# A hybrid encoder block on one core: next stage's factors made under the last products, tiles placed for that, one accumulator

## The chip, the cores and the metric

The kernel runs on one core of a Trainium2 chip. The metric is the device time of one execution in microseconds. Before the change it is 3190.73 us, the median of three executions (3188.22 to 3192.93).

The engines of a core work side by side, each on its own list of instructions in a fixed order: PE multiplies matrices, DVE, ACT and POOL work on elements, and SP's queue issues DMA transfers. An instruction waits until what it reads is written and what it overwrites has been read; everything behind it on its engine waits too.

## The reference

One layer of an encoder on a stream x of 2048 rows by 1024 columns, all in float32:

```python
xn = rmsnorm(h, g_pre_mix)
p = xn @ w_in                                   # 1024 -> 4608 columns
y_a = spatial_gating(gelu(p_a), ...) @ w_out_a   # gMLP in chunks of 128 rows
y_b = hyena_mixer(p_b, ...) @ w_out_b            # two long convolutions by FFT
m = (sigmoid(g_a) * y_a + sigmoid(g_b) * y_b) @ w_o
h = h + rmsnorm(m, g_post_mix)
hn = rmsnorm(h, g_pre_ffn)
f = square(relu(hn @ w_ff1)) @ w_ff2             # 1024 -> 4096 -> 1024
h = h + rmsnorm(f, g_post_ffn)
```

The change touches the last four lines, and the layout in which the result of the second convolution is stored.

## The kernel before

Every float32 product is made of three matmuls: each factor is split into a high part that PE takes at full rate (`_h`, a cast on ACT, line 36) and the rest (`_l`, a subtraction on DVE, line 42), and `mm3` (lines 47 to 49) adds h·h, l·h and h·l. The two halves together are called a factor here, and making them is called cutting it.

Four stages follow one another.
- Input projection, filters, FFT convolutions and gMLP, up to about 1434 us. The second convolution leaves its result in DRAM as `z2d`.
- **Merge**, to about 1765 us: for each of 8 blocks b of 256 rows, `project(b)` (products with w_out_b, gating) and then the products with w_o (tile `mo`). The rows are normalised, added to x on POOL, written to `hd`, normalised again (`rows_in`, tile `mx_n`, line 928), transposed by PE (`ta`, line 933), copied by ACT (`xb`), combined by DVE and written to `xtd`. The work on one block's rows is queued in the list `late` and interleaved with the next block's products; what is left for b = 7 runs at the end.
- **Up** (hn @ w_ff1), 33 steps s to about 2479 us. It uses a scheme of seven products in place of eight for 2x2 blocks. The right factors x[1..7] (`xh`, `xl`, from `xtd`) stay for 16 steps (q = s // 16 is the half of the rows), the left factors come from a pair of weight columns, one `raw8` buffer of 1 MB a step, by sums and differences. One product is 4 x 3 matmuls of 128x512 into one PSUM bank. Results (squared relu) are written to `sd`.
- **Down** (@ w_ff2), to about 3150 us: for c = 0..7 and n = 0..6 four products r = 0..3 of 12 matmuls, `s` (from `sd`) by `t` (from weight blocks `wr`). With c // 4 the half of the rows changes. At c % 4 = 0 ACT copies the bank into `acc[n, r]` (line 1244), later DVE adds (line 1246). After c % 4 = 3 `finish` combines the seven accumulators (line 1254), squares on ACT (1270), multiplies by the gain on POOL (1271), makes the reciprocal root by a chain of small DVE instructions, adds the rows of `hd` (1277) and writes `out` (1278).

The loads that matter go through SP: `load8` takes one of three 1 MB `raw8` buffers, for weight pairs, right factors and `sd` alike. A scheduler sets the order on each engine when the program is built, from the order of the code and the dependencies; a pool's tile waits for the last reader of the tile that held its memory before. In the up stage the right factors lie in pool `xc`, left ones in `fs` (5 buffers), rows in `fr`; the down stage opens its pools where those were.

Of the kernel before, what the change touches and what calls it, by code (L numbers as in the profile page):

```python
# [26 lines left out]
class Kernel:  # L27
# [174 lines left out]
    def prologue(self):  # L202
# [10 lines left out]
        self.gpm = load("gpm", [128, 8])  # L213
        dt = lambda name, shape, t=F32: d.tile(shape, t, name=name)
# [3 lines left out]
        self.z2d = dt("z2d", [4, 128, 32, 64])  # L218
# [326 lines left out]
    def gen_fft(self):  # L545
# [74 lines left out]
        for o in range(2):  # L620
# [76 lines left out]
            for j in range(18 if o == 0 else 16):  # L697
# [10 lines left out]
                if j < 16:  # L708
# [14 lines left out]
                    nc.vector.tensor_tensor(xi, y, xi, op=OP.mult)  # L723
                    zo[j] = xi
                    if o == 0:
                        late.append(lambda j=j, xi=xi: nc.sync.dma_start(
                            self.z1d[j].rearrange("p t n -> p (t n)"), xi))
                    else:
                        late.append(lambda j=j, xi=xi: nc.sync.dma_start(
                            self.z2d[:, :, 2 * j:2 * j + 2, :].rearrange("t p a n -> p t (a n)"), v4(xi)))  # L730
# [124 lines left out]
    def merge(self, st3):  # L855
# [9 lines left out]
        wsp = E("mw", 2)  # L865
        c = E("mc", 1)
# [3 lines left out]
        mtp = E("mt", 2)  # L870
        gpf = self.bcast(E("mf", 1), "gpf")
# [49 lines left out]
        def rows_in(b, i, x, bt):  # L921

            j = mp.tile([128, D], BF16, name="mx_j", bufs=1)
# [4 lines left out]
            nc.vector.scalar_tensor_tensor(xs, x, r, gpf, op0=OP.mult, op1=OP.mult)  # L928

            def turn(j):  # L930
# [5 lines left out]
                nc.scalar.copy(t, p)  # L936
                bt[j, i] = t
            late.append(lambda: turn(0))
            late.append(lambda: turn(1))
# [3 lines left out]
        def sums(b, bt):  # L943

            t1, t2, t4 = [xp.tile([128, Q], F32, name=f"xs{n}") for n in range(3)]
            sub = lambda o, a, c: nc.vector.tensor_tensor(o, a, c, op=OP.subtract)
            b11, b12, b21, b22 = bt[0, 0], bt[0, 1], bt[1, 0], bt[1, 1]
            sub(t1, b12, b11)
            sub(t2, b22, t1)
            sub(b12, b22, b12)  # L950
            sub(t4, b21, t2)
            c = slice((b % 4) * 128, (b % 4) * 128 + 128)
            for n, t in enumerate((b11, b21, t2, b12, t1, t4, b22)):
                nc.sync.dma_start(self.xtd[b // 4][n][:, :, c], t.rearrange("p (k n) -> p k n", k=4))
# [41 lines left out]
        for f in late:  # L996
            f()
# [441 lines left out]
```

## Time and profile before

| | us |
|---|---|
| median of three executions | 3190.73 (3188.22 to 3192.93) |
| the profiled execution | 3195.43 |
| its span in the trace | 3193.7 |
| PE busy in the span | 2890.2 (90%) |
| DVE busy | 2271.3 (71%) |
| ACT busy | 1523.4 (48%) |
| mean granted clock of PE | 0.961 |

A timeline row gives the start (us from the span's start), the time taken, the engine, the line of the kernel, the operation, output<-input tiles, and in brackets how long the engine had been idle and who released it. PE's matmuls overlap, so one that takes 0.39 us may start 0.23 us after the one before. The granted clock is a share of the full 2.4 GHz; 0.5 is the lower level of 1.2 GHz.

### The profile page before, as it was taken

To read this page: it belongs to the slowest core of one execution; us is meant where nothing else is said; L and a number is where in the kernel's file an instruction comes from. 1 tells how busy PE (TensorE), PEld (TensorE's weight loads), DVE (VectorE), ACT (ScalarE), POOL (GpSimd) and SP (SyncE) were. 2 spreads that over 40 slices of the span, in tenths; PEclk is the share of its full clock that TensorE was granted. 3 is DMA by queue.
4 is the path that set the end of the run, shared out by engine and by line. 5 is a ranking of instruction groups with operands and counts; after the bars stand their busy time and mean duration, and the time that the engine had idled before them with its cause. 6 is when DMAs were issued, how large, how long until landed. Compare 5 with 4: busy or idle time off the path is not lost. (4 is left out here: it accounts for less than half of the span.)

```text
span 3193.7 us, 37066 instructions
## 1 busy us (share of the span) xinstructions
PE 2890.2 (90%) x12910; PEld 2315.1 (72%) x12910; DVE 2271.3 (71%) x3532; ACT 1523.4 (48%) x2335; POOL 380.6 (12%) x324
## 2 busy tenths in 40 slices
PE   7999899998999899998999599968999799969994
PEld 5777766777777677787777488856888588848883
DVE  6589867777775866847776566656666567895788
ACT  4466555666535666324443444444444433334332
POOL 1122310211211211210111000000000000030002
PEclk9999999999999999999999799988999899979997
DMA  8556566454697454598866444444444544444332
GB/s 312 187 192 215 183 219 204 150 166 137 228 308 252 136 171 155 191 256 267 224 202 199 157 154 152 151 140 154 153 150 156 201 164 149 150 178 158 147 119 92
DMA packets 310952, 581.11 MB, mean 182 GB/s; under 512 B 58213, under 2 KB 147685, under 8 KB 292589
## 3 DMA queue, kind: packets, MB, share of 16 engines
q1 hardware_dynamic: 286348, 500.10, 47.3%
q10 hardware_dynamic: 19152, 61.35, 6.0%
q0 software_dynamic: 5264, 17.31, 1.4%
q8 instruction: 101, 1.65, 0.2%
q14 instruction: 87, 0.70, 0.1%
HBM read 385.72 MB, written 192.94 MB: 181 GB/s over the span
## 5 line engine op out<-in xcount | busy, mean ns | idle before, releaser
L36 ACT CAST s_h<-raw 128x512 fp32r<-128x512 f32 (+1 forms) x248 | 225.6, 911 | 539.5 <-PE mm L48 511.7
L47 PE MATMUL mm<-xh,w_hi 128*128 128x512 f32 x1152 | 459.8, 400 | 6.0 <-ACT xh L36 3.0
L48 PE MATMUL mm<-xl,w_hi 128*128 128x512 f32 x1152 | 457.3, 397 | 2.6 <-DVE xl L42 2.6
L49 PE MATMUL mm<-xh,w_lo 128*128 128x512 f32 x1152 | 457.8, 398 | 0.0
L47 PE MATMUL mm<-xh,s_h 128*128 128x512 f32 x896 | 360.1, 402 | 41.7 <-ACT xh L36 41.7
L47 PE MATMUL mm<-t_h,s_h 128*128 128x512 f32 x896 | 350.9, 393 | 36.0 <-ACT t_h L36 23.0
L48 PE MATMUL mm<-xl,s_h 128*128 128x512 f32 x896 | 360.6, 403 | 11.2 <-DVE xl L42 11.2
L48 PE MATMUL mm<-t_l,s_h 128*128 128x512 f32 x896 | 351.5, 392 | 18.2 <-DVE t_l L42 18.2
L42 DVE TENSOR_TENSOR s_l<-raw,s_h 128x512 fp32r<-128x512 f32 (+1 forms) x248 | 259.7, 1048 | 141.3 <-ACT s_h L36 141.0
L49 PE MATMUL mm<-xh,s_l 128*128 128x512 f32 x896 | 358.4, 400 | 0.0
L49 PE MATMUL mm<-t_h,s_l 128*128 128x512 f32 x896 | 351.1, 392 | 0.0
L47 PEld LDWEIGHTS mm<-xh,w_hi 128*128 128x128 f32 x1152 | 219.9, 191 | 60.1 <-ACT xh L36 5.4
L48 PEld LDWEIGHTS mm<-xl,w_hi 128*128 128x128 f32 x1152 | 219.7, 191 | 53.1 <-issue 4.5
L49 PEld LDWEIGHTS mm<-xh,w_lo 128*128 128x128 f32 x1152 | 219.5, 191 | 46.8 <-issue 2.0
L47 PEld LDWEIGHTS mm<-xh,s_h 128*128 128x128 f32 x896 | 172.4, 192 | 85.4 <-ACT xh L36 45.3
L1097 DVE TENSOR_TENSOR r<-r,mm 128x512 f32<-128x512 f32 x160 | 109.9, 687 | 164.4 <-PE mm L49 163.0
L47 PEld LDWEIGHTS mm<-t_h,s_h 128*128 128x128 f32 x896 | 170.1, 190 | 72.4 <-ACT t_h L36 23.4
L48 PEld LDWEIGHTS mm<-xl,s_h 128*128 128x128 f32 x896 | 172.3, 192 | 54.8 <-DVE xl L42 14.7
L1271 POOL TENSOR_TENSOR acc<-acc,gpo 128x512 f32<-128x512 f32 x32 | 49.0, 1558 | 1353.6 <-ACT pn_j L1270 1351.7
L48 PEld LDWEIGHTS mm<-t_l,s_h 128*128 128x128 f32 x896 | 169.8, 190 | 54.8 <-DVE t_l L42 19.3
L49 PEld LDWEIGHTS mm<-xh,s_l 128*128 128x128 f32 x896 | 172.7, 193 | 40.1
L49 PEld LDWEIGHTS mm<-t_h,s_l 128*128 128x128 f32 x896 | 169.7, 189 | 35.4
(274 smaller groups left out, 5762.1 us busy)
## 6 DMA issues: line engine op xcount, KB each, us to landing
sd<-r SPq DMA_DIRECT2D x224, 256.0 KB, 3.8
raw<-sd SPq DMA_DIRECT2D x56, 1024.0 KB, 4.8
w_raw<-in_win_dram ACTq DMA_DIRECT2D x101, 512.0 KB, 3.8
raw<-in_wf_dram SPq DMA_DIRECT2D x32, 1024.0 KB, 6.3
wr<-in_wf_dram SPq DMA_DIRECT2D x32, 1024.0 KB, 5.6
sk<-fs SPq DMA_DIRECT2D x64, 256.0 KB, 2.7
sf<-z_s SPq DMA_DIRECT2D x64, 256.0 KB, 3.5
z_raw<-sf SPq DMA_DIRECT2D x64, 256.0 KB, 2.8
```

The source lines that it names most:

```text
L36: nc.scalar.copy(hi, src)
L42: e.tensor_tensor(lo, src, hi.bitcast(F32), op=OP.subtract)
L47: mm(ps, a[0], b[0], start=start, stop=False, **kw)
L48: mm(ps, a[0], b[1], start=False, stop=False, **kw)
L49: mm(ps, a[1], b[0], start=False, stop=stop, **kw)
L1097: add = lambda o, a, b: nc.vector.tensor_tensor(o, a, b, op=OP.add)
L1271: nc.gpsimd.tensor_tensor(c[e], c[e], gpo[:, es], op=OP.mult)
```

## The change

- `ffn_start`, which runs under the last products of the merge, now also loads and cuts the first right factor (into a pool `x1` of its own) and two left ones. The work on the rows of b = 7 leaves the merge: `last_rows`, a generator run in steps 2 to 5 of up, loads the rows from `hd` again, normalises them, transposes them and writes `xtd`.
- The gain `g_pre_ffn` is applied after the transpose, by ACT, four copies of 128x128 with a scale (`gained`); before the transpose DVE multiplies by the root alone.
- In up, right factors of the first half are cut one by one ahead of the products that need them, those of the second half each after its last product in step 15 (4 and 3 in step 16). The pool `fs` has 3 buffers instead of 5.
- In down, `s` and `t` alternate between pools of one buffer placed on the right and left, and there is one `acc` tile. The additions of the combination follow the products from which they can be made (`ends`), the row-set (5, 4) is finished after n = 5 for all r, (1, 6) after n = 6 in pairs of r, one chain for the root for a batch. For the last half of the rows the (1, 6) finish works without POOL (`tail`).
- `z2d` is laid out so that the merge reads whole rows of 4 KB per partition; its writes are two of 256 B pieces instead of one of 512 B.

```diff
-        self.z2d = dt("z2d", [4, 128, 32, 64])
+        self.z2d = dt("z2d", [4, 128, 2, 32, 32])
...
-                    nc.sync.dma_start(zrs[-1][:, t], self.z2d[t, :, :, 8 * b:8 * b + 32])
+                    nc.sync.dma_start(zrs[-1][:, t], self.z2d[t, :, b // 4])
...
-            nc.vector.scalar_tensor_tensor(xs, x, r, gpf, op0=OP.mult, op1=OP.mult)
+            nc.vector.tensor_scalar(xs, x, r, None, op0=OP.mult)
...
-                nc.scalar.copy(t, p)
+                self.gained(t, p, j)
...
-                rows_in(b, i, x, bt)
+                if b < 7:
+                    rows_in(b, i, x, bt)
...
-        for f in late:
-            f()
...
+    def gained(self, t, p, j):
+        for k in range(4):
+            ks = slice(k * 128, k * 128 + 128)
+            self.nc.scalar.activation(t[:, ks], p[:, ks], AF.Copy, scale=self.gpf[:, 4 * j + k:4 * j + k + 1])
...
-        self.fs = R(self.fs_st, "fs", 5)
-        self.pairs = {}
+        self.x1p = R(self.fs_st, "x1", 1)
+        self.fs = R(self.fs_st, "fs", 3)
+        self.pairs, self.facs, self.x = {}, {}, {}
         self.load_pair(0)
         yield
+        self.xcut(self.x1p, 0, 1)
+        self.need(0, 1)
+        yield
+        self.load_pair(1)
+        self.need(0, 2)
+
+    def xcut(self, pool, p, i):
+        raw = self.load8(self.xtd[p][self.AT[i]], [128, 4, Q])
+        x = self.x[p, i] = pool.tile([128, 4, Q], F32R, name=f"xh{i}"), pool.tile([128, 4, Q], F32R, name=f"xl{i}")
+        self.split(*x, raw)
...
+        def last_rows():
+            raw = self.load8(self.hd[3][256:512, :].rearrange("(i p) d -> p i d", p=128), [128, 2, D])
...
+                        nc.tensor.transpose(p[:, k * 128:(k + 1) * 128], raw[:, i, ds], self.ident)
+                    bt[j, i] = row()
+                    self.gained(bt[j, i], p, j)
+                yield
+            self.sums(7, bt, [row() for n in range(3)])
...
+            nxt = lambda i: xcut(1, i) if s == 15 else None
+            if s == 2:
+                rows = last_rows()
+            next(rows, None)
             if s < 32:
-                if new:
-                    xcut(s // 16, 1)
                 d["a"] = bank()
-                product(d["a"], need(s, 1)[0], 1, True)
+                product(d["a"], need(s, 1)[0], q, 1, True)
+                nxt(1)
...
+            if s == 0:
+                xcut(0, 6)
             if s > 0:
-                product(st[s - 1]["c"], need(s - 1, 7)[5], 4, False)
+                self.load_pair(s + 1)
+                product(st[s - 1]["c"], need(s - 1, 7)[5], (s - 1) // 16, 4, False)
+                if s == 16:
+                    xcut(1, 4)
...
-        acc_p, sp, tp = E("acc", 1), E("sp", 2), E("tp", 2)
+        R = lambda name, bufs: E(name, bufs, side="right")
+        tp, sp = [R("tpa", 1)], [E("spa", 1)]
         wr = E("wr", 5)
+        sp.append(E("spb", 1))
+        tp.append(E("tpb", 1))
+        acc = E("acc", 1).tile([128, 7, 4, Q], F32, name="acc")
...
+        ends = {0: ((1, 0), (2, 0)), 2: ((3, 2), (6, 2)), 3: ((5, 3),), 4: ((6, 4), (4, 3))}
...
-                if c % 4 == 3 and n == 6:
-                    self.finish(acc, gpo, c // 4, r)
+                if last:
+                    for o, x in ends.get(n, ()):
+                        add(a(o), a(o), a(x))
+                    if n == 6 and r % 2 == 1:
+                        self.finish(acc, gpo, g, 0, (r - 1, r), g == 1)
+            if last and n == 5:
+                self.finish(acc, gpo, g, 1, range(4), False)
...
+                if not tail:
+                    nc.gpsimd.tensor_tensor(acc[:, at[e], r, :], acc[:, at[e], r, :], gpo[:, e * Q:e * Q + Q], op=OP.mult)
...
+                if tail:
+                    nc.vector.scalar_tensor_tensor(a, a, rd[:, m:m + 1], gpo[:, es], op0=OP.mult, op1=OP.mult)
+                    nc.vector.tensor_tensor(h[:, es], a, h[:, es], op=OP.add)
+                else:
+                    nc.vector.scalar_tensor_tensor(h[:, es], a, rd[:, m:m + 1], h[:, es], op0=OP.mult, op1=OP.add)
```

PE's order from the merge into up, before (`mo` is the product with w_o, `ta` a transpose, `mm` the first product of up):

```order
L47 MATMUL mo<-wo_h,mt_h 128x512
L933 MATMUL ta<-ident,mx_n 128x128 x4
L48 MATMUL mo<-wo_l,mt_h 128x512
L49 MATMUL mo<-wo_h,mt_l 128x512
L933 MATMUL ta<-ident,mx_n 128x128 x12
L47 MATMUL mm<-xh_16657,s_h 128x512
```

And after the change:

```order
L47 MATMUL mo<-wo_h,mt_h 128x512
L48 MATMUL mo<-wo_l,mt_h 128x512
L49 MATMUL mo<-wo_h,mt_l 128x512
L47 MATMUL mm<-xh_16517,s_h 128x512
L48 MATMUL mm<-xl_16518,s_h 128x512
L49 MATMUL mm<-xh_16517,s_l 128x512
```

The transposes of the last rows no longer stand between the two stages. SP's queue behind the last step of up, before (`raw8` loads of `sd` and `wr` are the factors of down, `nt_x` rows for its finish):

```order
L852 DMA gpo2_21724<-in_gpo2_dram 128x1024
L1265 DMA nt_x_23608<-hd0_122 128x1024
L1265 DMA nt_x_23637<-hd0_122 128x1024
L1021 DMA raw8_21813<-sd003_143 128x2048
L1094 DMA sd134_193<-r_21684 128x512
L1094 DMA sd132_191<-r_21685 128x512
L1094 DMA sd133_192<-r_21516 128x512
L1094 DMA sd136_195<-r_21686 128x512
L1021 DMA raw8_21882<-sd004_144 128x2048
L1207 DMA wr_21728<-in_wf2_dram 128x2048
```

And after:

```order
L1054 DMA raw8_21859<-sd002_144 128x2048
L1120 DMA sd135_196<-r_21730 128x512
L1120 DMA sd131_192<-r_21774 128x512
L859 DMA gpo2_21841<-in_gpo2_dram 128x1024
L1260 DMA wr_21845<-in_wf2_dram 128x2048
L1260 DMA wr_21849<-in_wf2_dram 128x2048
L1120 DMA sd134_195<-r_21794 128x512
```

The first two `wr` loads now follow the load of `gpo2` at once, which waits for the last product of up. DVE's order in the last step of c = 3, before (`pn_` tiles are the chain for the root):

```order
L1246 TENSOR_TENSOR acc_21756<-mm_23587,acc_21756 128x512
L1246 TENSOR_TENSOR acc_21756<-mm_23666,acc_21756 128x512
L1254 TENSOR_TENSOR acc_21756<-acc_21756 128x512 x5
L1273 TENSOR_TENSOR pn_s1_23617<-pn_ss_23610 128x1
L1254 TENSOR_TENSOR acc_21756<-acc_21756 128x512
L72 TENSOR_SCALAR pn_a_23619<-pn_s1_23617 128x1
L1246 TENSOR_TENSOR acc_21756<-mm_23745,acc_21756 128x512
```

And after:

```order
L42 TENSOR_TENSOR s_l_23790<-raw8_23651,s_h_23789 128x2048
L1301 TENSOR_TENSOR acc_21831<-mm_23797,acc_21831 128x512
L42 TENSOR_TENSOR t_l_23792<-wr_23653,t_h_23791 128x2048
L1301 TENSOR_TENSOR acc_21831<-mm_23811,acc_21831 128x512
L1058 TENSOR_TENSOR wr_23653<-wr_23939,wr_23653 128x2048
L1323 TENSOR_TENSOR pn_s4_23744<-pn_ss4_23719 128x4
L1301 TENSOR_TENSOR acc_21831<-mm_23867,acc_21831 128x512
```

The factors of the next half's first step (`s_l`, `t_l`) now stand among the last additions, and the additions of the combination are gone from there.

## Rows read from the trace of the kernel before

**Rows 1.** The profile's page, part 1: each engine's busy time, its share and its instructions.

```profile
PE 2890.2 (90%) x12910; PEld 2315.1 (72%) x12910; DVE 2271.3 (71%) x3532; ACT 1523.4 (48%) x2335; POOL 380.6 (12%) x324
```

**Rows 2.** `windows` view: stretch, its length, each engine's busy time (instructions), clock, DMA share, GB/s.

```profile
1750.00:1850.00 100.00, 66.87 (x257) 51.84 (x256) 62.71 (x111) 41.12 (x58) 5.47 (x4) 0.83 0.51 170
2000.00:2100.00 100.00, 100.00 (x432) 81.05 (x431) 66.17 (x101) 49.52 (x83) 0.00 (x0) 1.00 0.44 147
2100.00:2200.00 100.00, 63.49 (x231) 48.48 (x230) 52.64 (x64) 39.19 (x51) 0.00 (x0) 0.76 0.45 150
2450.00:2550.00 100.00, 76.78 (x324) 62.03 (x323) 47.97 (x39) 41.20 (x47) 0.00 (x0) 0.88 0.58 206
2600.00:2700.00 100.00, 100.00 (x442) 82.80 (x442) 72.61 (x59) 33.45 (x18) 0.00 (x0) 1.00 0.45 166
2800.00:2900.00 100.00, 69.03 (x283) 56.06 (x282) 78.02 (x137) 41.51 (x61) 25.25 (x15) 0.83 0.52 189
3150.00:3193.00 43.00, 0.50 (x3) 0.08 (x1) 36.12 (x109) 7.23 (x20) 16.14 (x13) 0.53 0.50 171
```

**Rows 3.** Timeline of PE around the merge's end: start, length, line, tiles, count, [wait before <-releaser].

```profile
1779.91 1.94 PE L933 MATMUL ta<-ident,mx_n 128*128 128x128 f32 x8 [14.61 <-DVE mx_n L928]
1791.70 0.80 PE L47 MATMUL mm<-xh,s_h 128*128 128x512 f32 x1 [5.97 <-ACT xh L36]
```

**Rows 4.** Timeline of PE in the middle of the up stage.

```profile
2142.49 0.80 PE L47 MATMUL mm<-xh,s_h 128*128 128x512 f32 x1 [14.56 <-ACT xh L36]
```

**Rows 5.** Groups by form on ACT and DVE (busy, mean ns | idle before), and DMA issues of the page.

```profile
L36 ACT CAST xh<-raw 128x2048 fp32r<-128x2048 f32 x14 | 26.5, 1894 | 26.6 <-DMA raw<-xt 26.6
...
L42 DVE TENSOR_TENSOR t_l<-wr,t_h 128x2048 fp32r<-128x2048 f32 x56 | 128.8, 2301 | 14.9 <-ACT t_h L36 14.9
L1025 DVE TENSOR_TENSOR wr<-wr 128x2048 f32<-128x2048 f32 x32 | 72.7, 2282 | 0.2
...
raw<-sd SPq DMA_DIRECT2D x56, 1024.0 KB, 4.8
```

**Rows 6.** Timelines of PE, SP's queue and ACT between up and down.

```profile
2501.61 2.08 PE L47 MATMUL mm<-t_h,s_h 128*128 128x512 f32 x4 [22.96 <-ACT t_h L36]
...
2492.39 2.03 SPq L1207 DMA_DIRECT2D wr<-in_wf_dram  x4
...
2499.66 1.90 ACT L36 CAST t_h<-wr 128x2048 fp32r<-128x2048 f32 x1 [17.11 <-DMA wr<-in_wf_dram]
```

**Rows 7.** Timelines of PE, DVE and POOL in the middle of down.

```profile
2839.38 0.79 PE L48 MATMUL mm<-t_l,s_h 128*128 128x512 f32 x1 [17.93 <-DVE t_l L42]
2865.56 0.80 PE L47 MATMUL mm<-t_h,s_h 128*128 128x512 f32 x1 [13.04 <-ACT acc L1244]
...
2818.76 1.79 DVE L1254 TENSOR_TENSOR acc<-acc 128x512 f32<-128x512 f32 x1
...
2820.81 0.68 DVE L1254 TENSOR_TENSOR acc<-acc 128x512 f32<-128x512 f32 x1
...
2814.51 5.49 POOL L1271 TENSOR_TENSOR acc<-acc,gpo 128x512 f32<-128x512 f32 x4 [0.61 <-ACT pn_j L1270]
```

**Rows 8.** Timelines of PE (its last matmul) and SP's queue at the end.

```profile
3150.11 0.39 PE L49 MATMUL mm<-t_h,s_l 128*128 128x512 f32 x1
...
3158.59 3.03 SPq L1278 DMA_DIRECT2D out_dram<-nt_x  x4
...
3187.08 3.68 SPq L1278 DMA_DIRECT2D out_dram<-nt_x  x4
```

**Rows 9.** Timeline of PE in the merge, and groups by form on DVE.

```profile
1440.76 0.38 PE L47 MATMUL mm<-zq_h,wb_hi 128*128 128x256 f32 x1 [3.26 <-ACT wb_hi L36]
...
1652.15 0.66 PE L933 MATMUL ta<-ident,mx_n 128*128 128x128 f32 x4 [1.58 <-DVE mx_n L928]
...
L928 DVE SCALAR_TENSOR_TENSOR mx_n<-mx,mx_y,gpf 128x1024 f32<-128x1024 f32 x16 | 20.5, 1284 | 1.7 <-DVE mx_y L67 0.2
...
L423 DVE TENSOR_SCALAR f_hd<-f_hd 128x512 f32<-128x512 f32 x8 | 3.4, 426 | 0.5
```

More of the change, by code (lines that the diff above doesn't have):

```diff
@@ L213, in prologue @@
         self.gpm = load("gpm", [128, 8])
+        self.gpf = load("gpf", [128, 8])
         dt = lambda name, shape, t=F32: d.tile(shape, t, name=name)
@@ L943, in sums @@
         def sums(b, bt):
[L945 to L954, printed above, removed]
+            self.sums(b, bt, [xp.tile([128, Q], F32, name=f"xs{n}") for n in range(3)])
         for b in range(8):
@@ L1120, in end_3 @@
             put(s, 3, n4)
-        facs = {}
-        def need(s, n):
-            if s < 32:
-                g = facs.setdefault(s, [self.left(s), []])
-                while len(g[1]) < n:
-                    g[1].append(next(g[0]))
-                return g[1]
+        def last_rows():
+            raw = self.load8(self.hd[3][256:512, :].rearrange("(i p) d -> p i d", p=128), [128, 2, D])
+            bt, s = {}, self.small.tile([128, 2], F32, name="lr_s")
+            for i in range(2):
+                j = rp.tile([128, Q], F32, name="r").bitcast(BF16)
+                nc.scalar.activation(j, raw[:, i], AF.Square, accum_out=s[:, i:i + 1])
+            r = self.rstd(self.small, s, 2, D, "lr")
+            for i in range(2):
+                nc.vector.tensor_scalar(raw[:, i], raw[:, i], r[:, i:i + 1], None, op0=OP.mult)
+            yield
+            for j in range(2):
+                for i in range(2):
+                    p = bank()
+                    for k in range(4):
+                        ds = slice((4 * j + k) * 128, (4 * j + k + 1) * 128)
+                        nc.tensor.transpose(p[:, k * 128:(k + 1) * 128], raw[:, i, ds], self.ident)
+                    bt[j, i] = row()
+                    self.gained(bt[j, i], p, j)
+                yield
+            self.sums(7, bt, [row() for n in range(3)])
+            yield
+        rows = iter(())
         for s in range(33):
+            q = s // 16
             new = s % 16 == 0 and s < 32
             d = st.setdefault(s, {})
-            self.load_pair(s + 1)
+            nxt = lambda i: xcut(1, i) if s == 15 else None
+            if s == 2:
+                rows = last_rows()
+            next(rows, None)
             if s < 32:
-                if new:
-                    xcut(s // 16, 1)
                 d["a"] = bank()
-                product(d["a"], need(s, 1)[0], 1, True)
+                product(d["a"], need(s, 1)[0], q, 1, True)
+                nxt(1)
                 d["u2"] = row()
@@ L1168, in up @@
             need(s, 4)
-            if new:
-                xcut(s // 16, 7)
+            if s == 0:
+                xcut(0, 5)
             d["c"] = bank()
-            product(d["c"], need(s, 4)[3], 7, True)
+            product(d["c"], need(s, 4)[3], q, 7, True)
+            nxt(7)
             d["u3"] = row()
@@ L1186, in up @@
             need(s, 6)
-            need(s + 1, 1) if s + 1 in self.pairs or s + 1 in facs else None
+            need(s + 1, 1)
+            if s == 0:
+                xcut(0, 3)
             need(s, 7)
@@ L1222, in cut @@
             src = (w(0, 0), w(1, 0), wraw.get((c, 2, 2)), wraw.get((c, 0, 1)), w(0, 0), w(1, 0), wraw.get((c, 1, 1)))[n]
-            s = sp.tile([128, 4, Q], F32R, name="s_h"), sp.tile([128, 4, Q], F32R, name="s_l")
-            t = tp.tile([128, 4, Q], F32R, name="t_h"), tp.tile([128, 4, Q], F32R, name="t_l")
+            s = [sp[k % 2].tile([128, 4, Q], F32R, name="s_" + x) for x in "hl"]
+            t = [tp[k % 2].tile([128, 4, Q], F32R, name="t_" + x) for x in "hl"]
             self.split(*s, sraw.pop(k))
@@ L1234, in down @@
             cut(k + 1)
-            if c % 4 == 0 and n == 0:
-                old, acc = acc, acc_p.tile([128, 7, 4, Q], F32, name="acc")
+            g, last = c // 4, c % 4 == 3
             s, t = fac.pop(k)
```

135 lines of the change are left out of this document (70 added, 65 removed).

## The prediction, made before the changed kernel ran

> **What bounds the kernel now.** I read the page's first part, then the windows, then the timelines at the places where the windows show PE short of work. PE is busy 90% of the span [rows 1], and in a full stretch nothing else limits it: 432 matmuls in 100 us of the up stage (0.231 us each), 442 in the down stage (0.226 us) [rows 2]. So the change can win only where PE runs short. There are five such places, and matmuls missing against a full stretch give their size [rows 2]:
> - merge to up: 432 - 257 = 175, by 0.231 us = **41 us**
> - middle of up, where the second half of the rows begins (s = 16): 432 - 231 = 201, **46 us**
> - up to down: 28.7 us at the one rate and 71.3 us at the other would be 439; 324 ran: 115, **26 us**
> - middle of down (c = 4): 442 - 283 = 159, **36 us**
> - tail: PE ends at 3150.5 [rows 8], the span at 3193.7: **43 us**
>
> Together 192 us. They hold the slow clock too: the granted clock is 0.76 to 0.88 there and 1.00 in full stretches [rows 2]. PE falls to its lower level after a wait and pays on after it (after the wait of 22.96 us four matmuls take 2.08 us [rows 6]).
>
> **Merge to up.** PE waits 14.61 us for the last block's normalised rows (mx_n), then 5.97 us for the first right factor [rows 3]; smaller waits for the next factors follow. The change takes the transposes of block 7 out of this place, cuts the first right and left factors under the last merge products, and PE goes from the last mo matmul into the first product. What is late next: the other six right factors. The raw8 pool has three 1 MB buffers, two hold pairs of weights, so five of the six loads pass through one buffer, each issued when the factor before it is cut. A round is a load of 4.8 us or a little more, a cast of 1.89 us and a subtraction of 2.3 us [rows 5]: 9 to 10.4 us. The second of these loads also stands on SP behind the two writes of hd3, which wait for POOL's last addition, some 6 us after the last mo matmul. Factor 2 is then whole at about 16 us, 7 at 26, 5 at 36, 4 at 47, and the ninth product ends at about 56 us, where nine products of 12 x 0.231 = 2.77 us are 25 us: 31 us lost, and some 2 us more for the clock. From 41 to 33: **gain 8** (3 to 14). The rows of block 7 are normalised in steps 2 to 5 instead: their 16 transposes are the same work, and the second half alone reads them.
>
> **Middle of up.** Now all seven factors are cut in the new half's first step; the longest wait is 14.56 us [rows 4]. In the new order factor i is cut as soon as its last product of the old half is done, over steps 15 and 16. The same round of about 10 us applies, but seven rounds (70 us) now have nearly two steps (14 products, 39 us) and the next step's first products to hide in. Followed through the order, factors 1, 6, 2 and 7 come before their products, 5 about 1 us late, 4 and 3 some 2 to 5 us each: 7 to 11 us, with the clock 8 to 16. From 46 to 12: **gain 34** (30 to 39).
>
> **Up to down.** PE waits 22.96 us; the weight loads (wr) are issued at 2492.39, 14 us after PE stopped, since they stand on SP's queue behind gpo2, two row loads, a raw load and the last writes of sd; t_h starts at 2499.66 [rows 6]. After: the pools are placed so that s_h, s_l are made early, but SP holds wr behind the load of gpo2, and that waits for the last up product. So wr is issued about 1 us after it, is usable 5 to 7.3 us later (the page's load; 2492.39 to 2499.66), cast 1.9 us: 8 to 10 us of wait in place of 22.96, and the same clock after it. **Gain 14** (8 to 18). Had the gpo2 load not stood there, the whole wait would be gone; that is the price of its place.
>
> **Middle of down.** PE waits 17.93 us for t_l, then 13.04 us for acc copies [rows 7]: DVE is finishing the first half of the rows, and the copies into the one acc tile wait for that. The change spreads 28 additions of 0.68 us [rows 7] over steps 0 to 4 of c = 3, and finishes two row-sets in three batches. In the steps with eight additions DVE has 2 x 2.3 + 4 x 0.68 + 8 x 0.68 = 12.8 us against PE's 48 x 0.226 = 10.8, so it comes some 2 us late by the end of c = 3. Then, from the end of step 5 to the t_l of c = 4, n = 2, DVE has 8 additions from PSUM (5.4), six subtractions for factors (13.8), three on weights (6.8), three small chains (3.5), four STT (3.0): 32.5 us. That equals PE's three steps, 32.5 us. What breaks the tie is POOL: its 16 multiplications run there. In the trace an addition takes 1.79 us while POOL is multiplying and 0.68 after it [rows 7]: 1.1 us per multiplication, 17 us in all. So about 17 us are lost in place of 36: **gain 19** (10 to 28). The copies of acc 1 wait, as before, for rows loaded through two buffers; by the order they come in time.
>
> The Trainium skill (SBUF — State Buffer, Who interferes with whom) says that DVE and GpSimd share a port pair as an exclusive lock, and that the later one blocks fully until the other's instruction ends. The trace agrees in kind, at 1.1 us of each multiplication's 1.37 (5.49 us for four). By the whole instruction the loss would be 22 us and this gain 14, inside the range.
>
> **Tail.** The writes of out go in four rounds, the first at 3158.59, the last at 3187.08 [rows 8]: 9.5 us a round, because a row buffer must be written out and loaded anew before it is used again. The change finishes rows (5, 4) after step 5 and the rest without POOL. The first round moves to about 1 us after PE's end instead of 8; but the four rounds through two buffers remain, a little shorter with DVE freer. PE's end plus 34 in place of 43, less 2 us for DVE's late steps of c = 7: **gain 7** (2 to 15).
>
> **Merge and the rest.** The row scaling becomes a tensor_scalar. A 128x512 one takes 0.426 us, so 128x1024 about 0.78 by the row for 128x512, against 1.284 for the STT now; PE waits 1.58 us for it once a block [rows 9]: 7 x 0.5 = **3.5**. The four scaled copies on ACT in place of one fill ACT's idle time, 0 (down to -3 if they delay casts). z2d is read in 4 KB pieces instead of 128 B: the wait of 3.26 us behind the load of wb_raw at 1440 [rows 9] may go: **3** (0 to 5). Written pieces halve, under products: 0.
>
> **Sum.** 8 + 34 + 14 + 19 + 7 + 3.5 + 3 = 88.5 us. The profiled execution took 3195.4 us, 4.7 above the median of 3190.7; by the median: **3102 us**.
>
> **Rivals.**
> - *The loads stay the limit.* Single-file rounds take longer beside the writes of sd and hd, and gains at the three load-bound places shrink to 2, 22 and 8, at mid-down to 10, tail 2, rest 2: 46, so 3145. For it: all three go through one or two raw buffers; against: DMA was busy only 0.45 to 0.58 there [rows 2]. 0.22, for times of 3120 to 3165.
> - *Everything hides.* Loads start a round earlier than I followed, the tail's rounds shrink: 15 + 40 + 20 + 28 + 18 + 8 = 129, so 3062. 0.15, for 3040 to 3080.
> - *Slower: too few factor buffers.* The pool for left factors goes from 5 to 3, so a factor is cast when the product two before its own ends, with one product (2.77 us) to spare. Cast and subtraction of 128x512 take about 1.3 us; but at each step's end DVE has six additions (4 us) queued ahead. If each of the 224 products came 0.4 us late, all 88 us would be gone; at 0.6 us: 3102 + 134 = 3236. By the order the tightest factor is whole about 0.5 us before its product. 0.05.
> - *The change does nothing at its places* (the waits only move): 3185 to 3197, 0.03.
>
> **Chances.** My forecast, 3080 to 3120, 0.55. Faster by over 0.2% (about what a measurement of this kernel can tell from no change) 0.92; within 0.2% 0.03; slower 0.05. The range, 3050 to 3145, leaves out the edges of both faster rivals and the slower one.
>
> **What would show it.** Right: no wait for mx_n at merge's end, then waits of 5 to 8 us for xh; at s = 16 waits under 5 us; 8 to 10 us for t_h between up and down; mid-down under 10 us each, DVE full; four rounds of writes at the end. Wrong: 100 us windows in up with fewer than 432 matmuls (factor buffers), or a wait for t_h near 20 us.

## The result and the profile after

The changed kernel takes 3113.38 us, the median of four executions (3106.96 to 3116.75), beside 3191.83 us for the kernel before in the same measurement: a ratio of 0.9751 with a 95% interval of 0.973 to 0.9772. The prediction was 3102 with a range of 3050 to 3145, so it was right, and its likeliest case (3080 to 3120) is the one that came. But the sum was right for partly wrong reasons, and the most useful finding of the study is a loss that no term of the sum had.

Part 1 of the profile's page of the changed kernel (engine, busy us, share, instructions) answers to [rows 1]. All engines have about as much to do as before; PE has as many matmuls in a span of 3105.2 us instead of 3193.7, and the mean granted clock is 0.981 instead of 0.961:

```profile
PE 2888.7 (93%) x12910; PEld 2302.1 (74%) x12910; DVE 2240.4 (72%) x3450; ACT 1535.7 (49%) x2431; POOL 374.2 (12%) x316
```

The windows of the changed kernel, with the columns of [rows 2]: merge to up, a full stretch of up, the middle of up, up to down, a full stretch of down, the middle of down, and the tail behind PE's end:

```profile
1750.00:1850.00 100.00, 79.53 (x298) 60.57 (x297) 64.98 (x104) 44.66 (x69) 7.54 (x4) 0.86 0.49 166
1950.00:2050.00 100.00, 100.00 (x431) 80.78 (x430) 64.80 (x101) 49.49 (x82) 0.00 (x0) 1.00 0.45 151
2080.00:2180.00 100.00, 94.36 (x395) 73.39 (x394) 74.47 (x101) 55.97 (x82) 0.00 (x0) 1.00 0.67 216
2420.00:2470.00 50.00, 39.92 (x163) 31.50 (x162) 33.35 (x25) 24.96 (x27) 0.00 (x0) 0.90 0.77 278
2600.00:2700.00 100.00, 100.00 (x435) 81.37 (x434) 79.92 (x70) 33.70 (x20) 0.00 (x0) 1.00 0.37 137
2740.00:2840.00 100.00, 90.98 (x383) 73.36 (x382) 77.23 (x83) 53.52 (x74) 31.92 (x16) 0.97 0.59 213
3075.20:3105.20 30.00, 0.01 (x1) 0.00 (x0) 20.12 (x52) 2.17 (x6) 0.00 (x0) 0.59 0.71 245
```

Against [rows 2], the short places have filled: 298 matmuls for 257 at the merge's end, 395 for 231 in the middle of up, 383 for 283 in the middle of down. The fifth row goes the other way: a full stretch of down, where PE waits for nothing and has the full clock, holds 435 matmuls where there were 442.

To see where the time went, I cut both traces at the same matmuls (counted from 0 at the start of each stage) and took the difference of their start times:

| stretch (us, profiled executions) | before | after | gain | predicted |
|---|---|---|---|---|
| start to the last `mo` matmul | 1764.5 | 1761.1 | 3.4 | 6.5 |
| to up's matmul 720 | 210.1 | 202.6 | 7.5 | 8 |
| up 720 to 1200 | 111.5 | 111.9 | -0.4 | 0 |
| up 1200 to 1560, the middle | 130.3 | 92.2 | 38.1 | 34 |
| up 1560 to 2640 | 251.0 | 251.8 | -0.8 | 0 |
| up 2640 to down 48 | 48.4 | 35.1 | 13.3 | 14 |
| down 48 to 1296 | 282.9 | 287.7 | -4.8 | 0 |
| down 1296 to 1632, the middle | 112.4 | 89.2 | 23.2 | 19 |
| down 1632 to PE's end | 239.5 | 243.6 | -4.1 | 0 |
| PE's end to the span's | 43.2 | 30.0 | 13.2 | 7 |

The six places gained 98.7 us, the full stretches gave back 10.1. That the rest, 88.6, is the predicted 88.5 is chance. By medians the gain is 78.5, ten short of the sum: the profiled execution of the changed kernel is the fastest of its four. In the profiles of the kernels below that have the same program up to the merge, the last `mo` matmul comes anywhere from 1757 to 1770 us; why was not examined. So the 3.4 us of the first row cannot be told from that scatter, and single kernels are compared below by their other stretches, which repeat within about 3 us in kernels that do not touch them.

PE's longest waits at each of the places from the merge's end on, one or two each, in the timeline of the changed kernel (start, length, line, tiles, [wait <-releaser]), answer to [rows 3, 4, 6, 7]:

```profile
1768.81 0.50 PE L48 MATMUL mm<-xl,s_h 128*128 128x512 f32 x1 [4.22 <-DVE xl L42]
1777.79 0.80 PE L47 MATMUL mm<-xh,s_h 128*128 128x512 f32 x1 [4.71 <-ACT xh L36]
...
2131.29 0.50 PE L47 MATMUL mm<-xh,s_h 128*128 128x512 f32 x1 [1.72 <-ACT xh L36]
...
2440.78 2.07 PE L47 MATMUL mm<-t_h,s_h 128*128 128x512 f32 x4 [9.83 <-ACT t_h L36]
...
2768.19 0.50 PE L48 MATMUL mm<-t_l,s_h 128*128 128x512 f32 x1 [3.31 <-DVE t_l L42]
2785.09 0.80 PE L48 MATMUL mm<-t_l,s_h 128*128 128x512 f32 x1 [5.71 <-DVE t_l L42]
```

The wait of 14.61 us for mx_n is gone, the middle of up has nothing above 2 us where it had 14.56, t_h comes after 9.83 instead of 22.96, and the middle of down waits 3.31 and 5.71 instead of 17.93 and 13.04.

### The profile page after: what moved, and what is told of

Its sections match the earlier page's. It is cut to its first block, busy times and chain, and to the rows that moved or that the text cites. A ratio compares the mean times of both kernels' runs of the same rounds, so it can differ in the third digit from the quotient of the medians.

```text
span 3105.2 us, 37077 instructions
## 1 busy us (share of the span) xinstructions
PE 2888.7 (93%) x12910; PEld 2302.1 (74%) x12910; DVE 2240.4 (72%) x3450; ACT 1535.7 (49%) x2431; POOL 374.2 (12%) x316
## 5 line engine op out<-in xcount | busy, mean ns | idle before, releaser
L1321 POOL TENSOR_TENSOR acc<-acc,gpo 128x512 f32<-128x512 f32 x24 | 42.0, 1782 | 1260.2 <-ACT pn_j L1319 1260.2
```

The source lines that it names most:

```text
L1321: nc.gpsimd.tensor_tensor(acc[:, at[e], r, :], acc[:, at[e], r, :], gpo[:, e * Q:e * Q + Q], op=OP.mult)
```

## Experiments

**Where the tiles stand.** Four rows of PE's timeline of the changed kernel in down: the first matmuls of two triples that follow one another, in an even step (first two rows) and in an odd one (last two):

```profile
2604.65 0.39 PE L47 MATMUL mm<-t_h,s_h 128*128 128x512 f32 x1
...
2605.35 0.39 PE L47 MATMUL mm<-t_h,s_h 128*128 128x512 f32 x1
...
2615.03 0.39 PE L47 MATMUL mm<-t_h,s_h 128*128 128x512 f32 x1
...
2615.71 0.39 PE L47 MATMUL mm<-t_h,s_h 128*128 128x512 f32 x1
```

Three matmuls take 0.70 us in the even step and 0.68 in the odd one. Apart from the steps in which PE waits, all even steps last 11.21 us, all odd ones 10.92, and in the kernel before every step lasted 10.88. No engine releases anything there. What differs is the memory: in even steps the program puts the weights (s) at byte 20864 of a partition and the streamed tile (t) at 188384; in odd steps they stand at 78208 and 94592; before, at 77664 to 110432 and 110432 to 143200. I took the theory that opposite ends of the memory cost time (A) against one in which something beside the even steps does (B), and moved only tiles.

One pool of the changed kernel moved:

```diff
-        tp, sp = [R("tpa", 1)], [E("spa", 1)]
+        tp, sp = [R("tpa", 1)], [R("spa", 1)]
```

> The changed kernel with one pool moved: the even steps' s tile of the down stage (spa) is placed on the right beside t, at bytes 172000 to 188384 of a partition, where before it stood at 20864 while its t stood at 188384. Theory A (a matmul whose weights and whose streamed tile lie on opposite ends of the partition's memory starts later): even steps of down fall from 11.21 us to 10.9, odd ones stay at 10.92; 28 x 0.3 = 8.4 us less in down. Theory B (the even steps are slow because of what other engines and transfers do beside them): even steps stay at 11.2. Either way s of step 0 now stands on memory that the last products of up read, so the wait between up and down (9.83 us) may grow by 0 to 4 us.

One pool of the kernel before moved, the other way:

```diff
-        acc_p, sp, tp = E("acc", 1), E("sp", 2), E("tp", 2)
+        acc_p, sp, tp = E("acc", 1), E("sp", 2), E("tp", 2, side="right")
```

> The kernel before with one pool moved: the t tiles of the down stage stand on the right (172000 to 204768), its s tiles stay at 77664 to 110432. Theory A: every step of down grows from 10.88 us to 11.1 to 11.3, so 55 steps cost 12 to 23 us. Theory B: steps stay at 10.88. The wait between up and down (22.96 us) may change by a few us in either theory, since t now waits for memory of the left factors.

Up's left factors moved to the side of their right factors (product 1 keeps its own, beside x1):

```diff
-        def cut(src):
-            h = self.fs.tile([128, 4, 128], F32R, name="s_h"), self.fs.tile([128, 4, 128], F32R, name="s_l")
+        def cut(src, first=False):
+            fs = self.fs if first or s == 0 else self.fs2
+            h = fs.tile([128, 4, 128], F32R, name="s_h"), fs.tile([128, 4, 128], F32R, name="s_l")
...
-        yield cut(a(0, 0))
+        yield cut(a(0, 0), True)
...
+        self.fs2 = E("fs2", 3)
```

> The changed kernel, up stage alone: from step 1 on the left factors of the products 6, 2, 7, 5, 4 and 3 stand in a pool of their own at 119168 to 131456, on the side of their right factors; those of product 1 stay at 174048 and beyond, beside x1 at 188384. Theory A: a full stretch of up falls from 0.233 us a matmul to 0.227, 31 steps x 84 matmuls x 0.006 = 16 us less; down is unchanged. Theory B: up stays at 0.233, total unchanged within 3 us.

The windows, each 100 us of full work: down with s moved beside t; down of the kernel before with t moved away from s; up with the left factors moved (the same window of the changed kernel is the second row of the windows above, 431):

```profile
2600.00:2700.00 100.00, 100.00 (x441) 82.42 (x440) 81.01 (x70) 34.25 (x19) 0.00 (x0) 1.00 0.37 137
```

```profile
2600.00:2700.00 100.00, 100.00 (x431) 80.42 (x430) 71.58 (x58) 33.37 (x18) 0.00 (x0) 1.00 0.41 155
```

```profile
1950.00:2050.00 100.00, 100.00 (x440) 82.39 (x439) 66.10 (x104) 51.94 (x85) 0.00 (x0) 1.00 0.43 148
```

Theory A holds three times, in both directions. With s moved, even steps take 10.94 us (435 to 441 matmuls, median 3106.82). In the kernel before, crossed (s on one side, t on the other), every step without a wait takes 11.15 to 11.2 (442 to 431), and it is slower by 0.46% (ratio 1.0046, interval 1.0028 to 1.0064, 3205.32 us), which is the predicted 12 to 23 us. With up's left factors moved, a matmul starts every 0.228 us on average instead of 0.233, and the median is 3092.42 (ratio 0.9692, 0.967 to 0.9714), 21 us below the changed kernel. Of the 19 us that its stretches of up give, 10 lie in the first one, more than the rate makes there (720 x 0.005 = 4); what gave the rest was not tried apart. So every kernel so far had a slow up stage, and the change added a slow half of down.

The trace of the changed kernel shows the same within one stage: product 1 is the only one of the seven with both operands on the right, and its 12 matmuls take 2.73 us (1986.07 to 1988.80), while the 12 of the crossed product behind it take 2.80 (to 1991.60); over steps 5 to 13 that is 0.227 us a matmul for product 1 and 0.234 for the other six. And one rest is left. In the kernel with up's left factors moved five products have 0.227, but product 1, which stays on the right, has 0.231, and product 4 behind it, back on the left, 0.230, though neither is crossed. In both, some nine matmuls behind the change of side take 0.224 to 0.237 us each before the spacing is back at 0.227. The kernel with s moved shows the same in down, where every step changes side (10.92 and 10.94 us instead of 10.88). What makes these slow was not tried.

**Between up and down.** The prediction said that without the load of gpo2 in front, the whole wait for t_h would be gone.

```diff
-        gpo = self.bcast(E("fg", 1), "gpo2")
+        fg = E("fg", 1)
...
         cut(0)
+        gpo = self.bcast(fg, "gpo2")
```

> The changed kernel with the load of gpo2 put behind the first weight loads of down. The prediction said that without this load in front of them the whole wait for t_h (9.83 us) would be gone. Rival: on SP's queue the two weight loads still stand behind a write of sd that waits for the last squares of up (issued at 2430.23, the weight loads at 2431.37), so they come at most 1 us earlier: wait of 8.5 to 9.5 us, total within 2 us of the changed kernel.

And on top of it the first weight loads on POOL's queue:

```diff
-                    nc.sync.dma_start(wraw[c, j, e], io["wf2"][c % 4, j, e])
+                    (nc.gpsimd if k < 3 else nc.sync).dma_start(wraw[c, j, e], io["wf2"][c % 4, j, e])
```

> As the kernel with gpo2 put late, and besides the first four weight loads of down are issued on POOL's own queue, where nothing stands before them. If the sd writes on SP's queue are what holds these loads (issued 0.3 us before PE's last product of up in the kernel with gpo2 late), they now go when the memory of factor 2 and 5 is free, 6 to 11 us earlier, t_h is there in time, and the wait of 7.29 us for it falls to under 2; the stretch from up's 2640th to down's 48th matmul goes from 32.6 to 23 to 26 us. Rival: the loads are held by the memory they write, which the last products read; the wait stays above 5 us.

SP's queue in the changed kernel, around PE's last product of up (which ends at 2430.95):

```profile
2427.42 3.13 SPq L1120 DMA_DIRECT2D sd<-r  x2
2430.99 0.33 SPq L859 DMA_DIRECT2D gpo<-in_gpo_dram  x1
2431.37 0.93 SPq L1260 DMA_DIRECT2D wr<-in_wf_dram  x2
```

The same with gpo2 late, where the last product ends at 2431.97:

```profile
2428.43 3.13 SPq L1120 DMA_DIRECT2D sd<-r  x2
2431.65 0.88 SPq L1260 DMA_DIRECT2D wr<-in_wf_dram  x2
```

PE's wait there:

```profile
2439.26 2.08 PE L47 MATMUL mm<-t_h,s_h 128*128 128x512 f32 x4 [7.29 <-ACT t_h L36]
```

And with the weight loads on POOL's queue: POOL, ACT and PE, where PE's last product ends at 2429.06:

```profile
2418.12 0.56 POOL L1260 DMA_DIRECT2D wr<-in_wf_dram  x1 [651.01 <-PE mm L49]
2423.74 1.58 POOL L1260 DMA_DIRECT2D wr<-in_wf_dram  x3 [5.07 <-PE mm L49]
...
2430.00 0.62 ACT L1116 ACTIVATE r<-r 128x512 f32<-128x512 f32 x1
2430.53 1.88 ACT L36 CAST s_h<-raw 128x2048 fp32r<-128x2048 f32 x1
...
2432.85 3.68 ACT L36 CAST t_h<-wr 128x2048 fp32r<-128x2048 f32 x2
...
2434.78 2.07 PE L47 MATMUL mm<-t_h,s_h 128*128 128x512 f32 x4 [5.72 <-ACT t_h L36]
```

The prediction's sentence was wrong. Without gpo2 the weight loads still stand behind two writes of sd, the second of which waits for the last squares: wait 7.29 us, stretch 32.6 instead of 35.1, median 3108.72 (the rival had the cause, but 8.5 to 9.5). On POOL's queue the first goes 11 us before PE's end and the other three 5, and still t_h comes late, by 5.72 us (stretch 32.0, hardly shorter, median 3103.95). The rival's wait above 5 us came, but not for its reason: the loads were not held to the end. Now ACT is in the way, which first squares up's last rows and cuts s for steps 0 and 1. Three waits stood one behind another, each a little shorter than the one ahead.

**Between merge and up.** Two edits, the second on top of the first:

```diff
-                nc.sync.dma_start(self.hd[b // 2][(b % 2) * B + i * 128:(b % 2) * B + (i + 1) * 128, :], x)
+                (nc.gpsimd if b == 7 else nc.sync).dma_start(self.hd[b // 2][(b % 2) * B + i * 128:(b % 2) * B + (i + 1) * 128, :], x)
```

> The changed kernel with the last block's two row writes (hd) issued on POOL's own queue, so that on SP the loads of right factors no longer stand behind them (in the changed kernel these two writes hold SP's queue from 1760.80 to 1770.25, and the next factor load goes at 1770.35). If the queue is what delays the second factor, its load goes 3 to 5 us earlier, every later round with it, and the stretch from the last mo matmul to up's 720th matmul (206.8 us in the changed kernel) becomes 202 to 204. Rival: the raw buffer is freed only by the cut of factor 6 at about 1766, and the rounds keep their pace: under 2 us.

```diff
-        raw = self.load8(self.xtd[p][self.AT[i]], [128, 4, Q])
         x = self.x[p, i] = pool.tile([128, 4, Q], F32R, name=f"xh{i}"), pool.tile([128, 4, Q], F32R, name=f"xl{i}")
+        raw = x[1].bitcast(F32)
+        self.nc.sync.dma_start(raw, self.xtd[p][self.AT[i]])
         self.split(*x, raw)
```

> As the kernel with POOL's row writes, and besides the right factors are loaded straight into the memory of their low halves (xl), cast from there and subtracted in place, so that no factor load passes through a raw buffer. If rounds through one raw buffer are what is left of the wait between merge and up (as the prediction reckoned, 33 us), the five late loads go at once after the last mo matmul, come whole one after the other about every 4 us, and the stretch from the last mo matmul to up's 720th matmul falls from 206.8 to 185 to 193 us. Rival: the five transfers of 1 MB share the DMA engines and all come late together, some 25 us after their issue: 200 to 207 us. In the middle of up each load now starts only after the factor's last product and is whole 9 us later, where 19 us are there: no new wait.

ACT's casts of right factors in the changed kernel (factors 6 and 2; 7, 5, 4 and 3 follow at 1785.93, 1794.97, 1804.66 and 1809.25), whose last `mo` matmul starts at 1761.08:

```profile
1762.15 1.90 ACT L36 CAST xh<-raw 128x2048 fp32r<-128x2048 f32 x1
...
1775.84 1.90 ACT L36 CAST xh<-raw 128x2048 fp32r<-128x2048 f32 x1 [10.69 <-DMA raw<-xt]
```

SP's loads of factors 2 and 7 in the kernel without the row writes (its last `mo` matmul starts at 1762.78; in the changed kernel these loads go at 1770.35):

```profile
1770.49 9.64 SPq L1054 DMA_DIRECT2D raw<-xt  x2
```

And with the loads in place: SP's queue, then ACT's first two casts:

```profile
1764.09 5.38 SPq L1042 DMA_DIRECT2D xl<-xt  x6
...
1770.31 1.90 ACT L36 CAST xh<-xl 128x2048 fp32r<-128x2048 f32 x1 [2.50 <-DMA xl<-xt]
1774.56 1.90 ACT L36 CAST xh<-xl 128x2048 fp32r<-128x2048 f32 x1 [2.35 <-DMA xl<-xt]
```

The row writes on SP's queue cost little: without them the stretch is 200.3 us instead of 202.6, where kernels that do not touch it have 202.0 to 205.2, since the raw buffer is free hardly sooner (median 3105.94): the load goes 7.7 us behind the last `mo` matmul instead of 9.3. The raw buffer was the limit: with the loads in place all six go within 5.4 us, the casts follow 2 to 5 us apart, where four of the five steps had been 9 to 14, the stretch falls to 179.2 us, more than either theory gave, and the median to 3087.72 (ratio 0.9666, 0.9645 to 0.9687). The 206.8 us from which both expectations set out were counted to a point 18 matmuls further on; by that count the two kernels have 204.5 and 183.4. In the middle of up the stretch is 93.4 us, 1.2 more than in the changed kernel and within the scatter.

**The middle of down.**

```diff
-                        self.finish(acc, gpo, g, 0, (r - 1, r), g == 1)
+                        self.finish(acc, gpo, g, 0, (r - 1, r), True)
...
-                self.finish(acc, gpo, g, 1, range(4), False)
+                self.finish(acc, gpo, g, 1, range(4), g == 0)
```

> The changed kernel with the first half's finish done without POOL, as the last half's is: 16 multiplications leave POOL, 16 additions come to DVE. The prediction put 17 us of the loss in the middle of down on POOL's multiplications slowing DVE. If that holds, DVE wins 16 x 1.1 and pays 16 x 0.65: the stretch from down's 1296th to 1632nd matmul falls from 89.3 us by 4 to 8, and the waits of 3.31 and 5.71 us for t_l shrink to under 2. Rival: what delays t_l is DVE's own queue of subtractions and additions, and ten microseconds more of it make the waits longer: the stretch grows by 2 to 8 us.

POOL and DVE in the changed kernel while POOL multiplies:

```profile
2744.91 29.36 POOL L1321 TENSOR_TENSOR acc<-acc,gpo 128x512 f32<-128x512 f32 x14 [2.04 <-ACT pn_j L1319]
...
2749.77 0.68 DVE L1301 TENSOR_TENSOR acc<-mm,acc 128x512 f32<-128x512 f32 x1
...
2757.72 1.26 DVE L56 TENSOR_SCALAR pn_t<-pn_a 128x4 int32<-128x4 int32 x1
...
2763.53 1.25 DVE L65 SCALAR_TENSOR_TENSOR pn_t<-pn_y 128x4 f32<-128x4 f32 x1
...
2764.77 3.37 DVE L42 TENSOR_TENSOR t_l<-wr,t_h 128x2048 fp32r<-128x2048 f32 x1
```

DVE at the same place of the program without POOL:

```profile
2762.42 0.16 DVE L65 SCALAR_TENSOR_TENSOR pn_t<-pn_y 128x4 f32<-128x4 f32 x1
2762.57 2.29 DVE L42 TENSOR_TENSOR t_l<-wr,t_h 128x2048 fp32r<-128x2048 f32 x1
```

The stretch falls from 89.2 to 82.1 us, 7.1 less and within the 4 to 8 expected; the waits for t_l fall to 2.08 and 2.12, a little over the expected 2 (median 3104.94). What the prediction priced for additions holds for other DVE instructions too: 1.1 us more, whether they have 4 columns (0.16 to 1.25) or 2048 (2.29 to 3.37). Not each one pays: some pay 0.5, others nothing. The small chain for the root, which the prediction counted at 3.5 us, paid most: between 2753 and 2775 us eight of its instructions took 1.25 us or a little more, and two subtractions 3.37. An addition with one input from PSUM stays at 0.68. The Trainium skill (SBUF — State Buffer, Who interferes with whom) says that a DVE instruction with two SBUF inputs contends with a GpSimd instruction that reads SBUF, and that one with a single SBUF input, outside the two-port modes, does not. The rows of 0.68, 1.25 (it reads pn_y twice) and 3.37 us agree. The row of 1.26 us has a single SBUF input, and so has another of the eight (at 2773.04): they would agree only if they ran in a two-port mode, which no run here shows.

**The tail.**

```diff
-        self.xp, self.junk = E("xp", 2), E("junk", 1)
+        self.xp, self.junk = E("xp", 3), E("junk", 1)
```

> The changed kernel with three row buffers instead of two in the finish of down (four do not fit beside the placed pools). The prediction said that four rounds of writes through two buffers set the tail; rounds are 8 us apart in the changed kernel (3075.27, 3083.41, 3091.66, 3098.89) and the span ends 30.0 us after PE. If the buffers set it, three rounds remain in the shadow of two and the end comes 4 to 8 us earlier after PE. Rival: the order on SP's queue (a load of rows behind the write before it) or DVE's own work sets the rounds: 0 to 2 us.

SP's queue behind PE's end, changed kernel (PE's end 3075.2), then three buffers (PE's end 3081.5):

```profile
3075.27 2.32 SPq L1337 DMA_DIRECT2D out_dram<-nt_x  x4
3083.41 2.51 SPq L1337 DMA_DIRECT2D out_dram<-nt_x  x4
3091.66 2.52 SPq L1337 DMA_DIRECT2D out_dram<-nt_x  x4
3098.89 3.34 SPq L1337 DMA_DIRECT2D out_dram<-nt_x  x4
```

```profile
3081.52 3.64 SPq L1337 DMA_DIRECT2D out_dram<-nt_x  x6
3090.99 4.07 SPq L1337 DMA_DIRECT2D out_dram<-nt_x  x6
3100.43 2.17 SPq L1337 DMA_DIRECT2D out_dram<-nt_x  x4
```

Three rounds instead of four, the end 24.2 us after PE instead of 30.0, as the buffers' theory said; median 3100.62.

**All edits together.** The kernel has the edits above, and in down both s and both t tiles at 20864 to 86400 and the weight buffers on the right:

```diff
-        tp, sp = [R("tpa", 1)], [E("spa", 1)]
-        wr = E("wr", 5)
+        wr = R("wr", 5)
+        sp, tp = [E("spa", 1)], [E("tpa", 1)]
         sp.append(E("spb", 1))
```

> All edits that helped, in one kernel: in-place loads of right factors and POOL's row writes; left factors of up on the side of their right factors; both s and both t tiles of down below byte 86400 and the weight buffers above 163808; gpo2 late and the first weight loads on POOL's queue; the first half finished without POOL; three row buffers. By the stretches of the single runs: 23 us between merge and up, 16 in up, 10 in down, 9 to 11 between the stages, 7 in the middle of down, 6 in the tail, together 71 to 73 us off the changed kernel's 3113: 3035 to 3045. Rival: gains overlap or the new placing opens a wait of its own (a weight load that now waits for the left factors' memory): above 3055.

The full stretches of up and down, whose places now all stand on one side:

```profile
1950.00:2050.00 100.00, 100.00 (x441) 82.39 (x440) 66.96 (x106) 52.24 (x85) 0.00 (x0) 1.00 0.41 145
2600.00:2700.00 100.00, 100.00 (x443) 82.81 (x442) 88.35 (x87) 36.41 (x23) 0.00 (x0) 1.00 0.40 150
```

It takes 3045.39 us (ratio 0.954, interval 0.9523 to 0.9558), 68 us below the changed kernel and 0.4 above what was expected. By stretches: 26.2 us between merge and up, 2.5 and 5.7 in full up, 5.5 between the stages, 4.8 and 4.1 in full down, 10.7 in its middle, 5.5 in the tail, and 1.4 lost in the middle of up, within the scatter. Single terms were off: 5.5 us between the stages where 9 to 11 were expected, and the full stretches of up gave 8 of the 16 booked for up. Two variants of it asked what was left there:

```diff
-        self.fs2 = E("fs2", 3)
+        self.fs2 = E("fs2", 5)
```

> The kernel with all edits, and in it five buffers instead of three for the left factors of up that stand on the left (from 119168 to 139648). This tests the prediction's rival that three buffers let left factors come late: in the kernel with all edits the step at the change of half still waits 3.19 us for s_h and 1.81 us for s_l, and the stretch from up's 1200th to 1560th matmul takes 93.6 us where 81.7 is the bare rate. If buffers hold those factors, the stretch falls to 85 to 90; if DVE's and ACT's queues hold them (seven right factors cut there too), it stays at 92 to 95, and full stretches of up stay at 0.228 us a matmul either way.

The middle of up fell from 93.6 to 85.4 us: here three buffers do hold left factors, but only at the change of half, as full stretches are the same. Yet the kernel is slower (3057.52), for a reason that I had not looked for: the two buffers push the row tiles up to byte 166272, over the first weight buffer of down at 163808, and its load, first in POOL's queue, now waits for up's last rows:

```profile
2398.50 2.10 POOL L1263 DMA_DIRECT2D wr<-in_wf_dram  x4 [634.16 <-DMA sd<-r]
...
2409.34 2.08 PE L47 MATMUL mm<-t_h,s_h 128*128 128x512 f32 x4 [24.76 <-ACT t_h L36]
```

Four buffers would not overlap; that was not run.

```diff
+            if k == 0:
+                self.split(*t, src)
             self.split(*s, sraw.pop(k))
-            self.split(*t, src)
+            if k > 0:
+                self.split(*t, src)
```

> The kernel with all edits, and in it, for step 0 of down alone, t is cut before s. After the weight loads were taken off SP's queue, t_h still comes 3.50 us late: on ACT its cast stands behind the cast of s and behind two squares of up's last rows, though its data have been there for over 10 us. If ACT's order is what is left, the wait for the first factor falls by 1 to 3 us (one cast of 1.88 us and one square less ahead of t_h; then s_h ends the wait); the stretch from up's 2640th to down's 48th matmul goes from 29.6 to 27 to 29 us. Rival: both factors are needed at once, so that the order of the two changes nothing: 29 to 30.

The stretch between the stages is 29.5 us, as before the edit: the rival holds, PE needs both factors, and first waits 3.50 us for s_h, then 2.02 for t_h. Its median of 3040.4 (ratio 0.9523, 0.9509 to 0.9537) is the lowest measured, 151 us below the kernel before, but its executions (3035.73 to 3046.02) overlap those of the kernel it is compared with (3042.75 to 3051.33).

## Why the prediction was right, and where it was not

- **Full stretches: a term that was missing.** That "in a full stretch nothing else limits it" was read as a constant, 0.231 us a matmul in up and 0.226 in down [rows 2]. The two rates were in front of me and I did not ask why they differ: up's tiles stand on opposite sides, down's did not. One of the signs that the prediction named, fewer than 432 matmuls in a window of up, came (431) and would have pointed at the factor buffers; moving the tiles gave 440. The change's placing crossed half of down's steps: 8.9 of the 10.1 us, shown in both directions by moving one pool; the other 1.2 us are in up, where six products run at 0.234 us a matmul and all ran at 0.232 before, and their cause is open.
- **Merge to up:** 7.5 for 8. The mechanism, rounds through one raw buffer, is shown by the loads in place. At the bare rate of the changed kernel, that of a full stretch without waits (720 x 0.233 = 168 us, and 3 for the moved transposes), 31 us are still lost in the stretch, where the prediction had 33. Single waits were smaller than the 5 to 8 us named as a sign, 4.71 at most. The row writes ahead on SP's queue, which it also named, cost some 2 us, which is within the scatter.
- **Middle of up:** 38.1 for 34, inside 30 to 39. At the bare rate 8 us are lost instead of 12; the longest wait for a right factor is 1.72 us, where 2 to 5 were booked for two of them.
- **Up to down:** 13.3 for 14, with a wait of 9.83 us in the forecast's 8 to 10. The weight loads went 0.4 us behind the last product, where about 1 was forecast, but what the gpo2 load costs was wrong: 2.5 us, not the whole wait, as the writes of sd and then ACT's casts stood behind it.
- **Middle of down:** 23.2 for 19. 12 us are lost instead of 17. The cause is shown: without POOL 7 of them go. The 17 us were 1.1 for each of 16 multiplications of 1.37 us; beside DVE's small instructions a multiplication took 2.1, and no DVE instruction paid more than 1.1 of it. What DVE paid in the trace is 8 x 1.1 on small instructions, 2 x 1.1 on subtractions and four times 0.5, 13 us. That this stands so close to the 12 lost is no proof of each share; the 7 us are what a run shows.
- **Tail:** 13.2 for 7. The four rounds remained, and buffers set them, but a round takes 8 us instead of 9.5, the first write goes 0.1 us after PE's end, and DVE's lateness, booked at 2 us, cost nothing.
- **Merge and the rest:** 3.4 for 6.5, but in these profiles the end of the merge moves by 13 us without a cause in the program. What repeats is the last block: from the last `mo` matmul of block 6 to that of block 7 it takes 28.8 us in all kernels with the change and 31.4 and 32.1 in the two without it; there four transposes of block 7 had stood, with a wait of 2.1 us for mx_n. That the seven blocks gained 0.7 is less than one block varies (39.7 to 40.9 us). mx_n did fall, to 752 ns from 1284 [rows 9], but the wait for it did not:

```profile
L934 DVE TENSOR_SCALAR mx_n<-mx,mx_y 128x1024 f32<-128x1024 f32 x14 | 10.5, 752 | 1.7 <-DVE mx_y L67 0.5
...
1650.93 0.66 PE L939 MATMUL ta<-ident,mx_n 128*128 128x128 f32 x4 [1.73 <-DVE mx_n L934]
```

In PE's order the first transposes of a block now stand ten `mo` matmuls before the second ones, where there were four; six matmuls of 0.227 us are 1.4 us, so PE comes to the shorter work earlier and waits as long. This is read from the order and the trace, and no run tried it alone. The wait at 1440 fell from 3.26 to 1.55 us.
- **The rivals.** The loads stayed the limit at the merge's end and, by their place in SP's queue, in part between up and down. Too few factor buffers: no lateness in full stretches; at the change of half it is real, 8 us in the kernel with all edits. Everything hides: it did not, 31, 8 and 12 us are still lost at three places, and the tail gained 13.2 of the 18 us that this rival gave it.

## What to carry to other kernels

Before a forecast takes a rate as given, ask why two stages of the same matmul have two rates; a change that moves pools can change it, and a window of full work, counted in matmuls, shows it where no wait does. When a wait has a named cause, look for what stands next behind it on each queue and engine: between up and down it was the load ahead, then the writes ahead, then the casts ahead. A buffer through which several loads pass one after another is best removed, here by loading into the memory that the result will have.

## What the hardware showed

- In the stages of this kernel a matmul of 128x512 at the full clock starts every 0.227 us when its weights and its streamed tile stand on the same side of a partition's memory, and every 0.231 to 0.237 us when one stands below byte 143,200 and the other above 172,000. Seen with both operands low (77664 with 110432), both high (172000 with 188384), and crossed either way. Distance alone is not it: in up of the changed kernel 110976 with 178144, at most 67,168 bytes apart and crossed, takes 0.234; in the merge of the kernel before, a streamed tile at 32608 to 65376 with weights at 138080, at least 72,704 apart and both low, takes 0.227. Behind a change of side some nine matmuls take 0.224 to 0.237 us even where none is crossed. Where between these bytes the border lies, why there is one, and whether the byte itself counts or what else lies in that part of the memory, was not tried.
- Beside a POOL multiplication, the DVE instructions that paid, all reading SBUF alone, mostly took 1.1 us more whatever their size (0.16 to 1.25, 2.29 to 3.37), and POOL's own multiplications took 2.1 us each (29.36 for 14), where four took 5.49 before [rows 7].
